# A float32 decoder trunk on one core: the activations of the 256-column matmuls 8 bytes further in SBUF

## The chip, the cores and the metric

The kernel runs on one core of one Trainium2 chip, in one launch. The metric is the device time of an execution in microseconds (us).

## What is computed

Two layers of a decoder trunk work on 256 tokens (S) of width 1,024 (D), in float32. In each layer:

```
h = rmsnorm(x) ;  proj = h @ w_in               (q, k, v of 24 heads of 64, three gates of width 1024)
o_a, o_b, o_c = dilated (12 heads), block (6), stick-breaking (6) attention
merged = g0*(o_a @ w_out_a) + g1*(o_b @ w_out_b) + g2*(o_c @ w_out_c)
x = x + merged @ w_o
x = x + square(relu(rmsnorm(x) @ w_up)) @ w_down      (width 4096)
```

A last RMSNorm follows.

## The kernel before

Every weight matrix is cut on the host into pieces of 128 x 1,024 values (512 KB), 140 for each layer, in the order of their use. SyncE loads them one after the other into four buffers `raw` (line 113). `split_one` (lines 123 to 134) parts each into a high half `wh`, which ScalarE writes (line 132), and a low half `wl`, the rest, which VectorE writes (line 133), six buffers each, three pieces ahead of their use. Activations are parted in the same way into a high and a low half. A product is then three matmuls: low weights by high activations, high by high, and high by low, added up in PSUM in the type float32r.

Three forms of these matmuls stand in the kernel:

- `proj` (lines 208 to 217): the weights are the stationary operand, 128 x 128, and 256 columns of activations (one k-tile of 128 channels, all tokens) stream through. For each of eight k-tiles there are three matmuls, lines 215, 216 and 217. The q, k and gate projections (`qk_pair`, `gate_tile`) read `xh`, the branch projections read `oT`, the projection `w_o` reads `mg`.
- `proj_wide` (lines 219 to 227), in the first half of the MLP: line 223 streams 512 columns (high and low half of `hl` side by side), line 226 streams the 256 of the high half.
- `v_chunk` (line 309) and `down_nat` (lines 668 to 670): the activations are stationary and 512 columns of weights stream.

The activations lie in two slots of 16,384 bytes in each partition, 8 k-tiles x 2 halves x 256 tokens x 4 bytes: a half of a k-tile takes 1,024 bytes. `hilo_slot(i, shift)` (lines 167 to 169) gives a view of slot i that begins `shift` elements behind its start. Slot 0 holds `hl` (shift 0: read by lines 223, 226 and 309) and, between two uses of it, `oT` (shift SHIFT = 16 elements, 64 bytes). Slot 1 holds `xh` and later `mg` (shift 0).

The order in SBUF is fixed by the lines 97 to 102, which allocate the tiles one behind the other: `hl0` (16,448 bytes, with room for the shift), `hl1` (16,384), `skip1` (192, never used), eight `ga` (3,072 each), six `wh` and six `wl` (4,096 each), `V`. The weights therefore begin 33,024 = 129 x 256 bytes behind the start of `hl0` (the `ga` take 96 x 256 more), and every 128 x 128 block of them at a multiple of 256 bytes from it. `hl` lies 0 bytes beyond such a multiple, `oT` 64 bytes, and `xh` and `mg`, at 16,448 = 64 x 256 + 64, also 64.

VectorE and ScalarE write these tiles: `xh` in `normalized` (lines 249 and 250), `oT` in `o_split` (365 and 366), `mg` in lines 599 and 600. Between the projections stand the units of attention; their scores are bursts of small matmuls (line 339), and their products of probabilities and values (line 374 among them) are single ones. The order of the instructions on each engine comes from the order of the program, with priorities for the splits (line 119) and the bursts (line 337).

Of the kernel before, what the change touches and what calls it, by code (L numbers as in the profile page):

```python
# [10 lines left out]
F32 = mybir.dt.float32  # L11
F32R = mybir.dt.float32r
# [3 lines left out]
P = 128  # L16
D = 1024
KT = D // P
S = 256
# [15 lines left out]
RPRI = 1000  # L35
NPRI = 0
NORM_AT = 3
SHIFT = 16
LATE_K = [range(0, 6), range(6, 8)]
BPRI = 400  # L40
QK_BUFS = 6
# [26 lines left out]
def trunk(ctx: ExitStack, tc: tile.TileContext, w, x, norms, gfin, consts, out):  # L68
# [10 lines left out]
    def T(tag, shape, bufs, dt=F32):  # L79
        uid[0] += 1  # L80
        return sp.tile(shape, dt, tag=tag, name=f"{tag}_{uid[0]}", bufs=bufs)
# [5 lines left out]
    def mm_bank():  # L87
        return PS("mm", [P, 512], 2)
# [4 lines left out]
    def t_bank():  # L93
        return PS("t", [P, 512], 2)


    for tag, shape, bufs, dt in (("hl0", [P, KT * 2 * S + SHIFT], 1, F32R),
                                 ("hl1", [P, KT * 2 * S], 1, F32R),
                                 ("skip1", [P, 48], 1, F32),
                                 ("ga", [P, 3, S], KT, F32),  # L100
                                 ("wh", [P, 1024], W_BUFS, F32R), ("wl", [P, 1024], W_BUFS, F32R), ("V", [P, 2, 8, 2, DH], 3, F32R)):
        T(tag, shape, bufs, dt)
# [47 lines left out]
    for o in START:  # L150
        if o[0] == "x":
            d = slice(int(o[1]), int(o[1]) + 2)
# [13 lines left out]

    def hilo_slot(i, shift=0):
        n = KT * 2 * S
        return T("hl%d" % i, [P, n + (SHIFT if i == 0 else 0)], 1, F32R)[:, shift:shift + n].rearrange("p (a b c) -> p a b c", a=KT, b=2)

    def norm_split(hl, nrm, d, on_dve=False):

# [56 lines left out]
    def by_residue(v):  # L229

        return v.rearrange("p (i r) -> p r i", r=DIL)

    hl = hilo_slot(0)
    for d in range(KT):
        norm_split(hl, 0, d, d == 0)

    postponed = []
    for layer in range(DEPTH):
        base = layer * PIECES
        xs = hl  # L240
        xh = hilo_slot(1)

        def normalized():

# [102 lines left out]
        def k_of(f, j, tokens):  # L347
            return QK[f][j * DH:j * DH + DH, 1, tokens]

        oT = hilo_slot(0, SHIFT)  # L350
        last_exp = [None]
        T0, T1, TT = slice(0, P), slice(P, S), slice(0, S)

# [211 lines left out]
        n = base  # L565
# [17 lines left out]
                act.preload_act_table_set("natural_log_exp_and_others")  # L583


        mg = hilo_slot(1)
        for d in range(KT):
            n = base + 60 + d
            st = s_bank()
# [13 lines left out]
        hl = hilo_slot(0)  # L603
        for d in range(KT):
# [6 lines left out]
            p = early[d] if d < 2 else mm_bank() if d % 2 else t_bank()  # L611
# [6 lines left out]
        n = base + 76  # L618
# [101 lines left out]
        hl = hilo_slot(0)  # L720
# [130 lines left out]
```

## Time and profile before

| | us |
|---|---|
| median of 3 runs | 864.6 (862.28 to 864.63) |
| the profiled execution | 864.01 |
| its span, first to last instruction | 862.3 |
| granted clock of TensorE, mean | 0.999 |

A busy share is the part of the span in which an engine works; the chain of work that ended last is followed back from the last instruction, at each step to what released it. For matmuls, which are pipelined, a duration is a latency that overlaps with the next one's; how fast they go one after the other is read from the starts in the timeline. PE is TensorE's matmul row and PEld its weight loads, DVE is VectorE, ACT is ScalarE. L215 is line 215.

### The profile page before, as it was taken

The numbers are of one execution on the slowest core, as the hardware profiler recorded it, in microseconds if no ns is written. First come the engines' busy times: TensorE is split into PE (matmuls) and PEld (weight loads), VectorE is DVE, ScalarE is ACT, GpSimd is POOL, SyncE is SP. The second block draws the span as 40 slices with busy tenths as digits, with TensorE's granted clock in tenths as the row PEclk, the third lists the DMA queues.
The fourth block names the chain that finished last, engine by engine and source line by source line (L and its number), as shares of the span: only waits on it lengthen the run. The fifth ranks groups of instructions, "written<-read, shape, count | busy, mean of one in ns | idle before, by whom it ended". The sixth has DMA issues, their size and how long they took to land.

```text
span 862.3 us, 15138 instructions
## 1 busy us (share of the span) xinstructions
PE 849.8 (99%) x6032; PEld 776.1 (90%) x6032; DVE 628.2 (73%) x958; ACT 468.2 (54%) x681; POOL 21.7 (3%) x36
## 2 busy tenths in 40 slices
PE   8999999999999999999999999999999999999996
PEld 6899999999998888888888999999999988888885
DVE  6977878855887766666578869796567967666664
ACT  6755656658364544444466665666574544444442
POOL 0000100000000000000000101010000000000000
PEclk9999999999999999999999999999999999999999
DMA  8875454554556566566567554445554665566541
GB/s 309 271 222 159 135 164 123 158 172 150 189 195 196 195 188 185 195 190 195 172 175 215 173 157 144 141 132 166 170 172 149 222 215 175 192 193 195 187 133 49
DMA packets 44375, 153.43 MB, mean 178 GB/s; under 512 B 5393, under 2 KB 5777, under 8 KB 44305
## 3 DMA queue, kind: packets, MB, share of 16 engines
q1 hardware_dynamic: 43872, 151.93, 55.9%
q8 instruction: 47, 0.77, 0.4%
q10 hardware_dynamic: 432, 0.54, 0.2%
q14 instruction: 24, 0.19, 0.1%
HBM read 149.31 MB, written 1.05 MB: 174 GB/s over the span
## 4 chain that ended last, share of the span: by engine, by line
PE 93%; DVE 3%; ACT 2%; issue 1%; DMA 1%; SPq 0%; POOLq 0%; DVEq 0%; ACTq 0%
PE mm L223 14%; PE mm L215 11%; PE mm L217 11%; PE mm L216 11%; PE mm L226 7%; PE s L668 7%; PE s L669 7%; PE s L670 7%; PE s L309 5%; PE s L339 2%; PE mm L309 2%; PE s L215 1%; PE s L217 1%; PE s L216 1%; PE t L215 1%
## 5 line engine op out<-in xcount | busy, mean ns | idle before, releaser
L133 DVE TENSOR_TENSOR wl<-raw,wh 128x1024 fp32r<-128x1024 f32 (+1 forms) x281 | 341.6, 1219 | 118.3 <-ACT wh L132 117.5
L132 ACT ACTIVATE wh<-raw 128x1024 fp32r<-128x1024 f32 (+1 forms) x281 | 294.9, 1054 | 238.1 <-PE mm L223 77.3
L215 PE MATMUL mm<-hl,wl 128*128 128x256 f32 x832 | 234.4, 282 | 0.0
L217 PE MATMUL mm<-hl,wh 128*128 128x256 f32 x832 | 233.1, 281 | 0.8 <-DVE hl L250 0.7
L216 PE MATMUL mm<-hl,wh 128*128 128x256 f32 x832 | 233.9, 281 | 0.0
L217 PEld LDWEIGHTS mm<-hl,wh 128*128 128x128 f32 x832 | 156.1, 188 | 1.8 <-DVE hl L250 1.2
L215 PEld LDWEIGHTS mm<-hl,wl 128*128 128x128 f32 x832 | 156.1, 188 | 1.2 <-issue 0.8
L216 PEld LDWEIGHTS mm<-hl,wh 128*128 128x128 f32 x832 | 156.2, 188 | 0.1
L223 PE MATMUL mm<-hl,wh 128*128 128x512 f32 x512 | 129.0, 392 | 0.3 <-DVE wk L640 0.3
L223 PEld LDWEIGHTS mm<-hl,wh 128*128 128x128 f32 x512 | 93.7, 188 | 18.4 <-DVE wk L640 0.5
L668 PE MATMUL s<-wl,ga 128*128 128x512 f32 x256 | 100.4, 392 | 0.0
L669 PE MATMUL s<-wh,ga 128*128 128x512 f32 x256 | 100.0, 391 | 0.0
L670 PE MATMUL s<-wh,ga 128*128 128x512 f32 x256 | 99.0, 389 | 0.0
L226 PEld LDWEIGHTS mm<-hl,wl 128*128 128x128 f32 x512 | 70.4, 190 | 5.3
L640 DVE TENSOR_REDUCE wk<-mm 128x256 f32<-128x512 f32 x64 | 44.0, 691 | 41.7 <-PE mm L226 41.7
L226 PE MATMUL mm<-hl,wl 128*128 128x256 f32 x512 | 72.0, 282 | 0.0
L670 PEld LDWEIGHTS s<-wh,ga 128*128 128x128 f32 x256 | 48.0, 188 | 10.2
L668 PEld LDWEIGHTS s<-wl,ga 128*128 128x128 f32 x256 | 48.2, 188 | 9.8 <-ACT wk L733 0.5
L669 PEld LDWEIGHTS s<-wh,ga 128*128 128x128 f32 x256 | 48.2, 188 | 8.8
L645 ACT ACTIVATE ga<-wk 128x512 fp32r<-128x512 f32 x32 | 20.2, 631 | 66.1 <-DVE wk L642 66.1
L215 PE MATMUL s<-hl,wl 128*128 128x256 f32 x128 | 36.1, 282 | 0.6 <-DVE wk L596 0.6
L216 PE MATMUL s<-hl,wh 128*128 128x256 f32 x128 | 35.7, 279 | 0.0
(153 smaller groups left out, 1001.2 us busy)
## 6 DMA issues: line engine op xcount, KB each, us to landing
raw<-in_w_dram SPq DMA_DIRECT2D x279, 512.0 KB, 3.6
V<-ga SPq DMA_DIRECT2D x32, 64.0 KB, 4.9
xres<-in_x_dram SPq DMA_DIRECT2D x4, 256.0 KB, 5.7
raw<-in_w_dram SPq DMA_DIRECT2D x2, 256.0 KB, 4.0
wk<-in_gfin_dram SPq DMA_DIRECT2D x2, 256.0 KB, 4.0
out_dram<-V SPq DMA_DIRECT2D x2, 256.0 KB, 2.3
out_dram<-V ACTq DMA_DIRECT2D x2, 256.0 KB, 2.1
c_maskA<-in_maskA_dram SPq DMA_DIRECT2D x1, 320.0 KB, 6.8
```

Of the source, the lines that this page charges most:

```text
L132: act.activation(hi[:, c:c + step], r[:, c:c + step], AF.Copy)
L133: dve.tensor_tensor(lo[:, c:c + step], r[:, c:c + step], hi[:, c:c + step].bitcast(F32), op=ALU.subtract)
L215: pe.matmul(dst, lo[:, c:c + P], hl[:, koff + k, 0], start=a, stop=False, skip_group_check=True)
L216: pe.matmul(dst, hi[:, c:c + P], hl[:, koff + k, 0], start=False, stop=False, skip_group_check=True)
L217: pe.matmul(dst, hi[:, c:c + P], hl[:, koff + k, 1], start=False, stop=z, skip_group_check=True)
L223: pe.matmul(bank, hi[:, k * P:k * P + P], hl[:, k].rearrange("p a b -> p (a b)"), start=k == 0, stop=False, skip_group_check=True)
L226: pe.matmul(bank[:, 0:S], lo[:, k * P:k * P + P], hl[:, k, 0], start=False, stop=k == KT - 1, skip_group_check=True)
L309: last_mm = pe.matmul(pv[t], xs[:, k, x_part, t * P:t * P + P], w_part[:, wsl], start=k == 0 and w_part is hi and x_part == 0, stop=k == K ...
L640: dve.tensor_reduce(t[:, a], p[a].rearrange("p (a b) -> p b a", a=2), axis=mybir.AxisListType.X, op=ALU.add)
L668: pe.matmul(dst, uh[:, j % 2, k], lo[:, c], start=j == 0, stop=False)
L669: pe.matmul(dst, uh[:, j % 2, k], hi[:, c], start=False, stop=False)
L670: return pe.matmul(dst, ul[:, j % 2, k], hi[:, c], start=False, stop=j == 2 * npairs - 1)
```

## The change

It gives both slots 128 bytes of room in place of 64 and 0, sets a skip of 128 bytes behind each, and lets `xh`, `oT` and `mg` begin 16 + STEP = 18 elements, 72 bytes, behind the start of their slot. `hl` stays at the start of slot 0. Slot 0 with its skip takes 16,640 = 65 x 256 bytes, slot 1 as much; the weights begin 33,280 = 130 x 256 bytes (and the `ga`) behind the start of `hl0`. So `xh`, `oT` and `mg` lie 72 bytes beyond a multiple of 256 from the weights, and `hl` 0 bytes.

```diff
-SHIFT = 16
+SHIFT = 32
+STEP = 2
...
     for tag, shape, bufs, dt in (("hl0", [P, KT * 2 * S + SHIFT], 1, F32R),
-                                 ("hl1", [P, KT * 2 * S], 1, F32R),
-                                 ("skip1", [P, 48], 1, F32),
+                                 ("skip0", [P, 32], 1, F32),
+                                 ("hl1", [P, KT * 2 * S + SHIFT], 1, F32R),
+                                 ("skip1", [P, 32], 1, F32),
...
     def hilo_slot(i, shift=0):
         n = KT * 2 * S
-        return T("hl%d" % i, [P, n + (SHIFT if i == 0 else 0)], 1, F32R)[:, shift:shift + n].rearrange("p (a b c) -> p a b c", a=KT, b=2)
+        return T("hl%d" % i, [P, n + SHIFT], 1, F32R)[:, shift:shift + n].rearrange("p (a b c) -> p a b c", a=KT, b=2)
...
-        xh = hilo_slot(1)
+        xh = hilo_slot(1, 16 + STEP)
...
-        oT = hilo_slot(0, SHIFT)
+        oT = hilo_slot(0, 16 + STEP)
...
-        mg = hilo_slot(1)
+        mg = hilo_slot(1, 16 + STEP)
```

## Rows read from the trace of the kernel before

**Rows 1.** The page: busy time, granted clock in 40 slices, chain by engine.

```profile
PE 849.8 (99%) x6032; PEld 776.1 (90%) x6032; DVE 628.2 (73%) x958; ACT 468.2 (54%) x681; POOL 21.7 (3%) x36
...
PEclk9999999999999999999999999999999999999999
...
PE 93%; DVE 3%; ACT 2%; issue 1%; DMA 1%; SPq 0%; POOLq 0%; DVEq 0%; ACTq 0%
```

**Rows 2.** Waits of the matmul row: us in total, times, longest.

```profile
PE mm L309 <- ACT wh L132: 2.2, 2, 1.1
...
PE mm L217 <- DVE hl L250: 0.7, 1, 0.7
```

**Rows 3.** Instructions of line 216: duration in ns, least, median and most.

```profile
L216 PEld LDWEIGHTS mm<-hl,wh x832: 187/188/193, 42.2 to 675.6; 128*128 128x128 f32 x167
L216 PE MATMUL mm<-hl,wh x832: 275/279/369, 42.3 to 675.7; 128*128 128x256 f32 x167
...
L216 PE MATMUL s<-hl,wh x128: 278/279/282, 196.4 to 655.7; 128*128 128x256 f32 x128
...
L216 PE MATMUL t<-hl,wh x64: 278/279/280, 219.6 to 672.9; 128*128 128x256 f32 x64
```

**Rows 4.** The page's groups: busy us, mean ns of one.

```profile
L215 PE MATMUL mm<-hl,wl 128*128 128x256 f32 x832 | 234.4, 282 | 0.0
L217 PE MATMUL mm<-hl,wh 128*128 128x256 f32 x832 | 233.1, 281 | 0.8 <-DVE hl L250 0.7
L216 PE MATMUL mm<-hl,wh 128*128 128x256 f32 x832 | 233.9, 281 | 0.0
...
L223 PE MATMUL mm<-hl,wh 128*128 128x512 f32 x512 | 129.0, 392 | 0.3 <-DVE wk L640 0.3
...
L668 PE MATMUL s<-wl,ga 128*128 128x512 f32 x256 | 100.4, 392 | 0.0
```

**Rows 5.** Timeline of the matmul row, 154 to 159: start us, us.

```profile
154.65 0.36 PE L216 MATMUL mm<-hl,wh 128*128 128x256 f32 x1
...
154.97 0.28 PE L215 MATMUL mm<-hl,wl 128*128 128x256 f32 x1
...
158.15 0.28 PE L215 MATMUL mm<-hl,wl 128*128 128x256 f32 x1
158.26 0.28 PE L374 MATMUL t<-ph,V 128*128 128x256 f32 x1
158.38 0.28 PE L216 MATMUL mm<-hl,wh 128*128 128x256 f32 x1
```

**Rows 6.** The same timeline, 115 to 119.

```profile
115.56 0.28 PE L215 MATMUL mm<-hl,wl 128*128 128x256 f32 x1
...
118.28 0.28 PE L215 MATMUL mm<-hl,wl 128*128 128x256 f32 x1
```

**Rows 7.** Groups of the matmul row in the stretch 115.6 to 118.2.

```profile
L215 PE MATMUL mm<-hl,wl 128*128 128x256 f32 x8 | 2.2, 276 | 0.0
L216 PE MATMUL mm<-hl,wh 128*128 128x256 f32 x8 | 2.2, 276 | 0.0
```

**Rows 8.** Timeline of the matmul row, 279 to 283, in the MLP.

```profile
279.29 1.98 PE L223 MATMUL mm<-hl,wh 128*128 128x512 f32 x8
281.10 1.12 PE L226 MATMUL mm<-hl,wl 128*128 128x256 f32 x8
282.05 0.86 PE L223 MATMUL mm<-hl,wh 128*128 128x512 f32 x3
```

**Rows 9.** Instructions of line 226.

```profile
L226 PEld LDWEIGHTS mm<-hl,wl x512: 187/192/192, 252.2 to 844.1; 128*128 128x128 f32 x171
L226 PE MATMUL mm<-hl,wl x512: 274/283/285, 252.4 to 844.2; 128*128 128x256 f32 x171
```

**Rows 10.** Busy us in two stretches: length, PE, PEld, DVE, ACT, POOL, then clock.

```profile
50.00:80.00 30.00, 30.00 (x334) 29.18 (x333) 25.34 (x46) 18.36 (x29) 2.90 (x4) 1.00 0.58 181
140.00:170.00 30.00, 30.00 (x257) 28.99 (x256) 25.73 (x76) 20.43 (x48) 1.22 (x2) 1.00 0.48 158
```

**Rows 11.** Waits of ScalarE.

```profile
ACT wh L132 <- PE mm L217: 50.1, 43, 2.2
```

## The prediction

> **What bounds the kernel now.** I read the page's first, second and fourth parts first. TensorE's matmul row is busy for 99% of the span, the chain of work that ended last lies on it for 93%, and the granted clock is at its full level in every slice, so the clock has nothing to give [rows 1]. The reader should see that the next engine, VectorE, is at 73% and holds 3% of the chain. The waits of TensorE come next: the longest kind sums to 2.2 us [rows 2]. So the time is the number of matmuls times the step from one matmul's start to the next, and only that step can be changed by moving addresses.
>
> The matmuls that the change moves are those of lines 215, 216 and 217: 832 + 128 + 64 on each line by the view of line 216, and as many on the other two lines, 3,072 in all [rows 3, 4]. Each streams 256 columns of activations while the weights of the following matmul are loaded. The recorded duration (about 280 ns) is a pipeline's latency; the step is read from the timeline, and it is there that the argument lies:
>
> - **The ordinary step.** From the start at 154.97 to the one at 158.15 there are 27 steps without a wait: 3.18 us / 27 = 117.8 ns [rows 5].
> - **A shorter step, with the same instructions and the same addresses.** After one matmul of line 374 came between, the same three lines go on from 158.38 [rows 5], and in another such stretch 24 steps take from 115.56 to 118.28: 2.72 / 24 = 113.3 ns [rows 6]. There the matmuls last 276 ns on average [rows 7], against a median of 279 on line 216 as a whole [rows 3].
> - **A longer step where the activations lie at distance 0.** Line 226 multiplies 256 columns too, but reads `hl` of slot 0, which lies a whole multiple of 256 bytes from the weights. Eight steps take from 281.10 to 282.05, 0.95 us. The first can use weights that were loaded under a 512-column matmul; if it takes 113 ns, the other seven take 0.837 / 7 = 119.6 ns [rows 8]. Its median duration is 283 ns, and its weight loads last 192 ns against 188 on line 216 [rows 3, 9].
> - **512 columns.** Eight steps take from 279.29 to 281.10, 226 ns each, twice the 113 ns [rows 8]. So 113 ns is what the stream of 256 columns takes when nothing holds it up, and the ordinary step holds 4.5 ns that are not streaming.
>
> Three steps (113.3, 117.8, 119.6) for one shape at one clock: the load of the next weights and the stream of activations get into each other's way, by an amount that hangs on how the two address sequences meet in time. [...]
>
> **The change part by part.**
>
> *The 8 bytes.* Two of the 256 elements are 2 x 113.3 / 256 = 0.9 ns of the stream. That is how far the stream's place is moved against the weight load. Distances 0 and 64 are the only ones that I find in the trace for these long runs; 72 is not shown, so its step is bounded by the nearest rows: 113.3 ns below, 119.6 ns above. I take the lower end. The reason is rows 5: an interruption by a single matmul moves these lines from 117.8 to 113.3 at unchanged addresses, and they stay there until something interrupts them. The collision is thus one of fine timing, and a shift by a part of a step can end it; a shift that only picks other places in memory while the timing is kept would not show two steps at one distance. That this shift goes the right way I can't read from a row, which is why the other cases keep nearly half the chance.
>
> The sum: 3,072 x (117.8 - 113.3) = 13.8 us if every one changed. Some run at 113.3 already [rows 6], and some stand beside a wait or beside a burst of small matmuls (line 216's mean of 281 against its median of 279 says that there are long ones [rows 3, 4]). I count nine tenths: 12.4 us.
>
> *What is late next.* The weights must be split by ScalarE and VectorE 4% faster. In the stretches with attention VectorE is busy for 25.34 and 25.73 of 30 us [rows 10]; in 4% less time that is 88 to 89%, no bound but little slack. ScalarE's splits on line 132 now wait for line 217 to give back a buffer, 50.1 us in total [rows 11]: the supply runs ahead and this wait shrinks first. I give back 1.5 us of the 12.4 for waits that this cover no longer hides everywhere; the bounds are 0 and 4 us.
>
> *What is written at the new addresses.* ScalarE and VectorE write `xh`, `oT` and `mg` 8 bytes further: 2 x 8 x 3 instructions in each layer, 96 in all. No row shows such a write at this offset. They stand off the chain; the one wait of TensorE on them (line 250) is 0.7 us [rows 2]. Cost 0, bounds half a microsecond either way.
>
> *What is not moved.* `hl` in slot 0 stays at a multiple of 256 from the weights, so lines 223, 226, 309 and 668 to 670 keep their steps. From the start of slot 0 to the weights it is now 33,280 bytes in place of 33,024, another whole multiple of 256; since lines 223 and 668 share a mean of 392 ns although their operands lie in different tiles [rows 4], I count that at 0. The tiles are larger by 256 bytes in a partition in sum, and no instruction touches the two skips. No instruction, transfer or wait is added.
>
> *Sum.* 12.4 - 1.5 = 10.9 us. The profiled execution took 864.0 us (span 862.3 and 1.7 around it), 0.6 below the median of 864.6. 864.0 - 10.9 = 853.1, and against the median 853.7: I say **854 us**.
>
> **The rivals.**
>
> *Nothing changes (0.26).* The step stays at 117.8 ns because the timing settles in the same way after each start, wherever the activations lie. For it: after a matmul that was held up (0.36 us at 154.65) the lines settle at the ordinary step again [rows 5]. Against it: distances 0 and 64 settle at different steps, so the address does enter. The time is 864.6, or a microsecond less or more.
>
> *The two streams meet worse (0.22).* At 72 bytes lines 215 to 217 fall to line 226's step. Place: each of the 3,072; price: nine tenths of them, 2,765 x (119.6 - 117.8) = 5.0 us, so 869.6. It decides as soon as the step passes 118.8, where 2.6 us are lost. For it: the distance 0 shows that an unlucky meeting is stable [rows 8]. Against it: nothing shows a distance that is no multiple of 64. [...]
>
> *The gain is there but halved (within the forecast).* If only every second stretch settles at 113.3, or the step ends near 115.5, the time is 858 to 859; that belongs to the first case's chance.
>
> **How the numbers follow.** A measurement of this kernel can tell 0.3%, 2.6 us, from no change: the line lies at 862.0 and at 867.2. The forecast has 0.52, all of it below 862.0; no change has 0.26, the worse meeting 0.22. The forecast's own range is 851 (all 13.8 us, none given back) to 860. The whole range takes in no change and the worse meeting at its price of 869.6: 851 to 870. What is left out is a step beyond line 226's, and a gain beyond the free stream's.
>
> **What would show it.** Right: long runs of lines 215 to 217 with 113.3 ns between starts, a median duration of 276 ns on line 216, weight loads still at 188; line 226 still at 283 and 512 columns at 389; and the loss of TensorE busy time all in the qk, gate and output projections, none in the MLP. Wrong: a median of 279 (nothing changed), or 282 and more with weight loads of 192 (they meet worse). The forecast also fails if the steps shorten and new waits for lines 132 and 133 before lines 215 to 217 take more than 4 us, or if lines 223 and 226 change their steps, since I hold that only the moved operand matters.

## The result and the profile after

The changed kernel took 873.02 us (median of 5 runs, 872.87 to 873.14) beside 864.6 of before on the same chip: ratio 1.0104, 95% interval 1.009 to 1.0118. It is slower by 1%, where I had forecast 1.2% faster, and it lies above the range of 851 to 870.

The page of the profiled execution (span 871.4 us, 9.1 more than before): busy time, granted clock, and the chain by engine, to be held against [rows 1].

```profile
PE 860.9 (99%) x6032; PEld 787.3 (90%) x6032; DVE 629.2 (72%) x958; ACT 468.1 (54%) x681; POOL 21.3 (2%) x36
...
PEclk9999999999999999999999999999999999999999
...
PE 97%; DVE 1%; DMA 1%; ACT 0%; issue 0%; SPq 0%; POOLq 0%; DVEq 0%; ACTq 0%
```

TensorE is still all there is, at the same clock and with the same number of instructions; it is busy for 11.1 us more, and no other engine for more than 1. The groups say which matmuls (line numbers are two higher now: 217 to 219 were 215 to 217, 225 was 223, 228 was 226, 670 was 668); busy us and mean ns, against [rows 4]:

```profile
L217 PE MATMUL mm<-hl,wl 128*128 128x256 f32 x832 | 238.3, 287 | 0.0
L219 PE MATMUL mm<-hl,wh 128*128 128x256 f32 x832 | 237.7, 287 | 0.7 <-DVE hl L252 0.7
L218 PE MATMUL mm<-hl,wh 128*128 128x256 f32 x832 | 235.3, 283 | 0.0
L225 PE MATMUL mm<-hl,wh 128*128 128x512 f32 x512 | 129.0, 392 | 0.3 <-DVE wk L642 0.3
L670 PE MATMUL s<-wl,ga 128*128 128x512 f32 x256 | 100.4, 392 | 0.0
L228 PE MATMUL mm<-hl,wl 128*128 128x256 f32 x512 | 72.0, 282 | 0.0
```

The three lines whose operand was moved went from 281 or 282 to 283 to 287 ns; the lines that read `hl` or stream weights stand where they stood, to the last digit. The timeline of the matmul row gives the step (start us, us):

```profile
203.09 0.28 PE L217 MATMUL mm<-hl,wl 128*128 128x256 f32 x1
...
205.13 0.28 PE L219 MATMUL mm<-hl,wh 128*128 128x256 f32 x1
```

Seventeen steps in 2.04 us are 120.0 ns, against 117.8 in [rows 5]. Within each three the lines now differ, as the groups of the stretch from 204 to 210 show (mean ns before the second bar):

```profile
L217 PE MATMUL mm<-hl,wl 128*128 128x256 f32 x16 | 4.5, 284 | 0.0
L219 PE MATMUL mm<-hl,wh 128*128 128x256 f32 x16 | 4.5, 284 | 0.0
L218 PE MATMUL mm<-hl,wh 128*128 128x256 f32 x16 | 4.4, 278 | 0.0
```

Over the whole trace I count the steps from the starts of all 3,072 matmuls and set apart those of 128 ns and more, which hold a wait or a change to small matmuls. Before: 2,976 steps of 117.6 ns on average, and 114 of them below 115.5. After: 2,976 steps of 120.8 ns, and one below 115.5. 2,976 x 3.2 ns = 9.5 us; the long steps give back 0.7. All steps of other lines together are 482.8 us before and 483.1 after. So the whole loss lies in the step of the moved matmuls. No wait of the matmul row was added. That of line 309 for ScalarE's split shrank from 2.2 to 1.0 us, and that of line 215 on line 596, 0.6 us before, is gone.

### The profile page after: what moved, and what is told of

Its sections match the earlier page's. It is cut to its first block, busy times and chain, and to the rows that moved or that the text cites. A ratio compares the mean times of both kernels' runs of the same rounds, so it can differ in the third digit from the quotient of the medians.

```text
span 871.4 us, 15138 instructions
## 1 busy us (share of the span) xinstructions
PE 860.9 (99%) x6032; PEld 787.3 (90%) x6032; DVE 629.2 (72%) x958; ACT 468.1 (54%) x681; POOL 21.3 (2%) x36
## 4 chain that ended last, share of the span: by engine, by line
PE 97%; DVE 1%; DMA 1%; ACT 0%; issue 0%; SPq 0%; POOLq 0%; DVEq 0%; ACTq 0%
PE mm L225 13%; PE mm L219 12%; PE mm L217 12%; PE mm L218 11%; PE mm L228 7%; PE s L670 7%; PE s L671 7%; PE s L672 7%; PE s L311 5%; PE s L341 2%; PE s L217 2%; PE mm L311 2%; PE s L219 2%; PE s L218 2%; PE t L217 1%; PE t L219 1%
## 5 line engine op out<-in xcount | busy, mean ns | idle before, releaser
L135 DVE TENSOR_TENSOR wl<-raw,wh 128x1024 fp32r<-128x1024 f32 (+1 forms) x281 | 341.9, 1220 | 123.3 <-ACT wh L134 123.1
L219 PE MATMUL mm<-hl,wh 128*128 128x256 f32 x832 | 237.7, 287 | 0.7 <-DVE hl L252 0.7
L217 PE MATMUL mm<-hl,wl 128*128 128x256 f32 x832 | 238.3, 287 | 0.0
L218 PE MATMUL mm<-hl,wh 128*128 128x256 f32 x832 | 235.3, 283 | 0.0
L218 PEld LDWEIGHTS mm<-hl,wh 128*128 128x128 f32 x832 | 159.4, 192 | 0.1
L219 PEld LDWEIGHTS mm<-hl,wh 128*128 128x128 f32 x832 | 157.4, 189 | 1.7 <-DVE hl L252 1.1
L225 PEld LDWEIGHTS mm<-hl,wh 128*128 128x128 f32 x512 | 93.7, 188 | 18.4 <-DVE wk L642 0.5
L228 PE MATMUL mm<-hl,wl 128*128 128x256 f32 x512 | 72.0, 282 | 0.0
```

The lines of the kernel that those rows point to most:

```text
L135: dve.tensor_tensor(lo[:, c:c + step], r[:, c:c + step], hi[:, c:c + step].bitcast(F32), op=ALU.subtract)
L217: pe.matmul(dst, lo[:, c:c + P], hl[:, koff + k, 0], start=a, stop=False, skip_group_check=True)
L218: pe.matmul(dst, hi[:, c:c + P], hl[:, koff + k, 0], start=False, stop=False, skip_group_check=True)
L219: pe.matmul(dst, hi[:, c:c + P], hl[:, koff + k, 1], start=False, stop=z, skip_group_check=True)
L225: pe.matmul(bank, hi[:, k * P:k * P + P], hl[:, k].rearrange("p a b -> p (a b)"), start=k == 0, stop=False, skip_group_check=True)
L228: pe.matmul(bank[:, 0:S], lo[:, k * P:k * P + P], hl[:, k, 0], start=False, stop=k == KT - 1, skip_group_check=True)
```

## The experiments

The question was what 72 bytes do to the step that 64 don't. Two answers stood against each other at first: that it is the **distance** between activations and weights, by the way in which the two address sequences meet in time (my prediction's reason), or that it is the **place** of the streaming operand alone: the remainder of its start, in bytes, by 16, which is 0 at 64 and 8 at 72. That it should be 16 was a supposition at first; what the step is at each place is shown by the maps alone (means of 118.2, 121.7, 120.3 and 118.1 ns at places 0, 4, 8 and 12, e8_map2). The expectations call the first the meeting or distance theory and the second the place theory. By the line of a place they mean the 16 bytes from one multiple of 16 to the next, a way to name addresses; no run shows a structure of the memory behind it. A third, the layout theory, has it that the new order of the tiles costs the time and the 8 bytes don't. The trunk is the whole kernel. Since the time of the whole kernel mixes many stretches, I also measured the step by itself, in kernels that run only these matmuls.

### A map of the step over the distance

```diff
+WOFFS = [0]
+REPS = 3
...
+    for wo in WOFFS:
+        for o in OFFS:
+            run(p, wo, o)
```

`OFFS` is the list of the distances, 0 to 60 bytes by 4, 64 to 240 by 16 and 248, and back again. `run` issues the three matmuls of lines 215 to 217 for eight k-tiles, REPS times, with the activations `o` and the weights `wo` elements of 4 bytes behind the start of their tiles.

> This kernel leaves out the trunk: it splits one piece of weights and one block of activations, and then runs the three matmuls of lines 215 to 217 for 8 k-tiles, three times over (72 matmuls), at each of 29 distances between activations and weights (0 to 60 bytes in steps of 4, 64 to 240 in steps of 16, 248), up the list and down again; nothing waits. [...] Meeting theory (the step depends on how the two address sequences meet in time): 120 ns at 0, 117.6 at 64, 120.8 at 72 as in the trunk, and other values from 113 to 124 between them that don't go by multiples of 16 alone. If distance did not matter in itself (layout theory), one value of about 117.6 everywhere.

Starts in the timeline of the matmul row, in pairs that are 60 steps apart: at 64 and 112 bytes on the way up, at 8, 4 and 0 on the way down.

```profile
156.64 0.28 PE L102 MATMUL mm<-hl,wl 128*128 128x256 f32 x1
...
163.71 0.28 PE L102 MATMUL mm<-hl,wl 128*128 128x256 f32 x1
...
182.34 0.28 PE L102 MATMUL mm<-hl,wl 128*128 128x256 f32 x1
...
189.14 0.28 PE L102 MATMUL mm<-hl,wl 128*128 128x256 f32 x1
...
489.20 0.28 PE L102 MATMUL mm<-hl,wl 128*128 128x256 f32 x1
...
496.40 0.28 PE L102 MATMUL mm<-hl,wl 128*128 128x256 f32 x1
...
497.87 0.29 PE L102 MATMUL mm<-hl,wl 128*128 128x256 f32 x1
...
505.27 0.29 PE L102 MATMUL mm<-hl,wl 128*128 128x256 f32 x1
...
506.72 0.28 PE L102 MATMUL mm<-hl,wl 128*128 128x256 f32 x1
...
513.92 0.28 PE L102 MATMUL mm<-hl,wl 128*128 128x256 f32 x1
```

7.07 us / 60 = 117.8 ns at 64, 6.80 / 60 = 113.3 at 112, 120.0 at 8, 123.3 at 4 and 120.0 at 0. These are the steps of [rows 5, 6, 8] and one worse. (72 was not in this list; the later maps have it.) The other distances, over the last 59 steps of each stretch: 4, 20, 36 and 52 bytes have 123.4, 122.3, 121.1 and 120.0 ns; 8, 24, 40 and 56 have 120.0, 120.0, 119.9 and 117.8; 12, 28, 44 and 60 all have 117.6 to 117.8. The multiples of 16 scatter from 113.3 to 120.0, and some have two values: 192 was 117.8 on the way up and 113.3 on the way down, with nothing changed but what ran before. Neither answer covers this alone: places 4, 8 and 12 have values of their own, but place 12 costs no more than many at place 0.

### The same map with the weights moved too

```diff
-WOFFS = [0]
+WOFFS = [2]
```

> The same map, but the weights too begin 8 bytes further, so that the distance is 8 less than the offset of the activations. [...] Meeting theory: the same curve against the distance, moved by 8 bytes: 117.6 ns at offset 72 (distance 64), 120 ns at offset 8 (distance 0).

The weights begin two elements, 8 bytes, further. Where the two answers differ, the place wins. Offset 20 (distance 12) has 121.1 ns; the first map had 122.3 at offset 20 and 117.7 at distance 12. Offset 12 (distance 4) has 117.7, against 117.7 at offset 12 and 123.4 at distance 4. The other offsets that are no multiple of 16 come within 1.3 ns of the first map at the same offset, but for 40 and 56, which differ from it by 1.9 and 2.2. At the multiples of 16 the values moved, by up to 7 ns: there the distance matters as well (96 had 120.0 in the first map, here 113.3 on the way up and 120.0 on the way down). Offset 48 (distance 40) had 113.3 on both ways.

### The offset back to 64, and on to 80, in the kernel

```diff
-STEP = 2
+STEP = 0      (e3_step0)
+STEP = 4      (e4_step4)
```

> The changed kernel with the offset set back from 72 to 64 bytes, all else of the new layout kept (room, skips, slot 1 and the weights 192 and 256 bytes further). [...] Layout theory: it stays near 873 us.

863.26 us beside 863.1, ratio 1.000 (0.9991 to 1.001), steps of 117.6. The new layout, with slot 1 and the weights further away, costs nothing; the 8 bytes alone are the change.

> The changed kernel with 80 bytes in place of 72: the next multiple of 16. [...] Meeting theory: not bound to that; the value that the first map gives for 80, between 855 and 875 us.

867.91 us beside 863.1, ratio 1.0053 (1.0036 to 1.007), steps of 119.2 on average. So the place alone does not give the step: 80 and 64 are both at place 0, and 80 is slower. The map had 120.0 there.

### Place 12 and place 4

```diff
-STEP = 2
+STEP = 3      (e7_76: 76 bytes)
+STEP = 1      (e9_68: 68 bytes)
```

> The changed kernel with 76 bytes in place of 72, which too begins inside a 16-byte line. [...] The place within the line decides, as in the first map (12, 28, 44 and 60 bytes all near 117.7 ns, 8, 24 and 40 near 120): about 117.7 ns and 864.5 us within 2.

864.67 us in a single run beside 864.03, steps of 117.7: 76 is no multiple of 16 either, and it loses nothing against 64. So there is no one price for every start off a multiple of 16.

> The changed kernel with 68 bytes in place of 72: the place inside a 16-byte line is 4. Place theory: slower still, since the maps have a mean of 121.8 ns at place 4 (120 to 124): 2,976 steps x (121.8 to 123.4 less 117.6) = 12 to 17 us over before, 876 to 881 us. Distance theory, in which the place in a line means nothing: no such order; a value between 113 and 124 that fits none of 72, 76 and 80 better.

872.89 us in a single run beside 863.77, steps of 121.0. The order (68 and 72 slow, 76 as 64) is that of the place; the size is below the 876 to 881 that I expected, since the trunk's stretches did not settle at the map's worst values.

### The maps again, with interruptions

```diff
+    for again in range(2):
+        for o in range(0, 64, 4):
+            for piece in range(3):
+                for n in range(4):
+                    pe.matmul(p[:, S:S + 64], wh[:, n * P:n * P + P], hl[:, 0:64], start=True, stop=True, skip_group_check=True)
+                run(p, 0, o, 1)
```

This second part runs every multiple of 16 bytes, three times and twice over, each time 24 matmuls behind four small ones of 64 columns.

> The first map for 64 to 128 bytes in steps of 4 and for 192, up and down, and then every multiple of 16 from 0 to 240 twice, each three times for 24 matmuls behind four small ones of 64 columns. Place within the line: about 120 ns at 72, 88, 104 and 120, 117.7 at 76, 92 and 108, over 120 at 68 and 84. In the second part, if the rhythm hangs on how a stretch begins, 24 matmuls at one distance have several values; 112 is of use to the trunk only if it stays near 113 to 115 there.

By a slip the list of distances went to the weights too, so that the first part ran every one of 18 offsets of the activations against every one of 18 of the weights, 1,296 stretches of 72 matmuls. That gives more than was asked. Mean steps in ns by the place of the activations, over all places of the weights (from the 21st matmul of a stretch on; the first three stretches left out):

```
place  stretches  mean   least   most
  0       431     118.2  113.3  123.4
  4       287     121.7  120.0  124.1
  8       287     120.3  117.8  123.3
 12       288     118.1  116.6  122.2
```

The place of the weights makes no such order (for each place of the activations, the means at place 0, 4, 8 and 12 of the weights agree within 0.7 ns). Each place of the activations met all four places of the weights, so the table parts the place from the distance. Only place 0 ever has 113.3, in 24 of 431.

In the second part, with interruptions, the last 20 steps of each stretch give this: 112 bytes had 115.0 to 115.3 ns in six of six, 192 had 113.5, 114.0 and 117.8, 64 had 117.8 in all six, 80 had 118.5 to 120.0, and the other multiples of 16 lay between 116.7 and 120.0. This orders the trunk's results: 64 at 117.6, 80 at 119.2, and the next two.

### 112 and 192 bytes in the kernel

```diff
-STEP = 2
+STEP = 12     (e5_112)
+STEP = 32     (e11_192, with more room and larger skips)
```

> The changed kernel with 112 bytes in place of 72. The first map held 113.3 ns at 112 on both ways through the list. If the map carries over to the trunk: about 2,900 of the 3,072 steps fall from 117.6 to 113.3, 12 us less than before, 851 to 854 us. If the trunk's interruptions throw the matmuls into another rhythm each time (the map had two values at 96 and 192), a mixture: 855 to 866 us.

856.23 us beside 864.03, ratio 0.9919 (0.9902 to 0.9935): the mixture, and not the 851 to 854 of a map carried over whole. 2,282 steps are below 115.5 ns, the mean is 114.6. The groups, and the longest waits of the matmul row:

```profile
L217 PE MATMUL mm<-hl,wl 128*128 128x256 f32 x832 | 232.5, 280 | 0.0
L218 PE MATMUL mm<-hl,wh 128*128 128x256 f32 x832 | 232.2, 279 | 0.0
L219 PE MATMUL mm<-hl,wh 128*128 128x256 f32 x832 | 231.2, 279 | 0.9 <-DVE hl L252 0.8
```

```profile
PE mm L311 <- ACT wh L134: 2.1, 2, 1.2
PE s L217 <- DVE wk L598: 1.2, 4, 0.4
```

Means of 279 and 280 against 281 and 282 in [rows 4]; the wait of line 215 on line 596 (now 217 and 598) is 1.2 us. The steps of 128 ns and more sum to 22.9 us, against 21.3 before: the weights keep up, and 1.5 us come back as waits and changes.

> The changed kernel with 192 bytes in place of 72 (place 0 of a line; room and skips larger). The first map held 117.8 ns on the way up and 113.3 on the way down there. Map carried over: a mixture, 852 to 866 us. Place theory alone bounds it from above only: not slower than before by more than a few us, since place 0 has a mean of 118.2 in the maps.

859.29 us beside 863.77, ratio 0.9947 (0.9932 to 0.9962): 1,493 steps below 115.5 and the rest near 117.6, the mixture that the map had.

### hl moved too

```diff
-    hl = hilo_slot(0)
+    hl = hilo_slot(0, 16 + STEP)      (three places, STEP = 12)
```

> As the run before, and hl too lies 112 bytes beyond a multiple of 256. If the map holds for line 226 (256 columns, 512 of them, at 120 ns), these fall to about 113.5: up to 3 us less than the run before. If what matters on line 226 is something else than the distance, no change against the run before, within 1 us.

857.24 us, 1.0 more than with `hl` at 0, where I had expected up to 3 less or no change. Line 226's step does fall, from 120 to 117.0, which is 1.5 us; but line 223's mean step rises from 229.8 to 231.6 (512 of them, 0.9 us), and line 309, where `hl` is the stationary operand, from 227 to 233 in the greater part. What is gained with one form is lost with two others.

### Weights moved in the kernel

```diff
+        o = 2                                              (e10_72_w8: all pieces, STEP = 2)
+        o = 2 if 12 <= n % PIECES < 76 else 0              (e12_48_w8: projections alone, STEP = -4)
         hi = T("wh", [P, 1088], W_BUFS, F32R)[:, o:o + 1024]
         lo = T("wl", [P, 1088], W_BUFS, F32R)[:, o:o + 1024]
...
```

The lines without a sign stand so in both; the tiles of the weights have room for the shift, and two small buffers are fewer.

> The changed kernel, and every piece of weights too lies 8 bytes further, so that the distance is 64 again while activations (and the weights, where they stream) begin at place 8 of a line. Two small buffers are fewer to make room, so only the steps count. Distance theory: lines of the 256-column matmuls back at 117.6 ns. Place theory: they stay at 120 to 121. [...]

877.47 us in a single run beside 863.77. The distance is 64 again, and the steps stay at 120.1 ns: the distance answer falls. The lines that stream weights at place 8, with 512 columns, are slower too. The groups, mean ns against the 392 of line 668 in [rows 4] and, last, against the 392 of line 223 there:

```profile
L672 PE MATMUL s<-wh,ga 128*128 128x512 f32 x256 | 101.4, 396 | 0.0
L671 PE MATMUL s<-wl,ga 128*128 128x512 f32 x256 | 101.3, 396 | 0.0
L673 PE MATMUL s<-wh,ga 128*128 128x512 f32 x256 | 101.1, 397 | 0.0
L226 PE MATMUL mm<-hl,wh 128*128 128x512 f32 x512 | 130.1, 394 | 0.3 <-DVE wk L643 0.3
```

The mean step of lines 668 to 670 (here 671 to 673) is 233 to 235 ns, against 228 to 230 before, and none is below 228, where before the ordinary one was 226 or 227. So streams of 512 columns lose 3 to 7 ns. That this is the place is not shown: their distance to `ga` moved by the same 8 bytes, and line 223 (here 226), whose stream `hl` stayed at place 0 while its stationary weights moved by 8 bytes, went from 229.8 to 231.9 ns.

> Activations at 48 bytes and, for the pieces of the 256-column projections alone, weights 8 bytes further (two small buffers fewer). The maps held 113.3 ns at this distance of 40 bytes with activations at place 0 in six of six stretches. Map carried over: steps near 113.5, 852 to 856 us. If the trunk's interruptions decide: 117 to 119 ns and 862 to 868 us.

855.44 us beside 863.77, ratio 0.9907 (0.989 to 0.9923), the best kernel of this study: 2,587 steps below 115.5 and a mean of 114.1. The matmul row's busy time fell as the step did:

```profile
PE 840.4 (98%) x6032; PEld 766.3 (90%) x6032; DVE 629.5 (74%) x958; ACT 468.0 (55%) x681; POOL 21.6 (3%) x36
```

### The same streams beside shorter loads

```diff
-                pe.matmul(p[:, 0:S], wl[:, c:c + P], ...
+                pe.matmul(q, wl[:, c:c + wide], ...
```

`wide` is 128, 64 and 32 columns of weights; `q` is as many partitions of `p`.

> This kernel leaves out the trunk, as the first map: the three matmuls over and over, 72 at each of 16 distances from 64 to 124 bytes in steps of 4, up and down, with weights of 128 columns, then of 64, then of 32 (a shorter load beside the same stream of 256 columns; nothing waits). Own cost: a stream that begins at place 4 or 8 of a 16-byte line takes longer by itself, so with 32 columns, where the load ends early, steps at place 4, 8 and 12 stay above those at place 0, by 2 ns or more where 128 columns show 120 to 123. Collision alone: with 64 and 32 columns the steps fall to 113.3 ns at every place, and the differences shrink with the load's length. With 128 columns the means of the maps should come again: about 122 at place 4, 120 at 8, 117.7 at 12.

Starts in pairs that are 60 steps apart: first with loads of 128 columns at 72 bytes, then with 32 columns at 68, 72, 76 and 112.

```profile
36.18 0.28 PE L103 MATMUL mm<-hl,wl 128*128 128x256 f32 x1
...
43.38 0.28 PE L103 MATMUL mm<-hl,wl 128*128 128x256 f32 x1
...
576.57 0.28 PE L103 MATMUL mm<-hl,wl 128*32 128x256 f32 x1
...
583.82 0.28 PE L103 MATMUL mm<-hl,wl 128*32 128x256 f32 x1
...
585.26 0.28 PE L103 MATMUL mm<-hl,wl 128*32 128x256 f32 x1
...
592.34 0.28 PE L103 MATMUL mm<-hl,wl 128*32 128x256 f32 x1
...
593.74 0.28 PE L103 MATMUL mm<-hl,wl 128*32 128x256 f32 x1
...
600.80 0.28 PE L103 MATMUL mm<-hl,wl 128*32 128x256 f32 x1
...
670.68 0.28 PE L103 MATMUL mm<-hl,wl 128*32 128x256 f32 x1
...
677.48 0.28 PE L103 MATMUL mm<-hl,wl 128*32 128x256 f32 x1
```

120.0 ns at 72 with the full load; beside loads of a quarter of the columns 120.8 at 68, 118.0 at 72, 117.7 at 76 and 113.3 at 112. Over all distances with 32 columns: place 4 has 120.3 to 121.8, place 8 117.8 to 120.1, place 12 116.6 to 117.8, place 0 113.3 to 117.6. With a full load the same places have 120.6 to 122.7, 118.8 to 121.4, 117.7 to 120.0 and 113.3 to 120.1; place 12, at a mean of 119.3, is above the 117.7 that I had expected. The means at places 0, 4, 8 and 12 are 116.9, 121.9, 120.2 and 119.3 with 128 columns, 116.5, 120.9, 119.8 and 117.6 with 64, and 115.5, 121.0, 119.1 and 117.4 with 32.

The load of a quarter of the columns lasts more than a quarter of the time (mean ns before the second bar):

```profile
L103 PEld LDWEIGHTS mm<-hl,wl 128*128 128x128 f32 x768 | 146.8, 191 | 15.8 <-ACT hl L95 15.8
L103 PEld LDWEIGHTS mm<-hl,wl 128*32 128x32 f32 x768 | 84.2, 110 | 7.2
```

A price that grew with the load's time would thus fall to about six tenths. Over 113.3 ns, the mean price at place 4 goes from 8.6 to 7.7 ns and at place 8 from 6.9 to 5.8: five sixths and more stay. Measured from the mean of place 0 with the same load, place 4 costs 5.0 ns with the full load and 5.5 with the shortest, and place 8 3.3 and 3.6, so that nothing shrinks. So the price at these places does not go by the length of the load. That the stream is slower by itself is the likeliest reading but not shown, since every matmul here has a load beside it, and a fixed price for each load would look the same.

## Why the prediction was wrong

**The step that failed** is the one that chose the end of the range: "I take the lower end." 113.3 ns was the right lower bound, and the sum behind it was sound, but the reason to take it was not. From one interruption that moved the lines from 117.8 to 113.3 ns I read that any shift by part of a step may end the collision. The runs show two things in its place. At place 0 the steps settle anywhere from 113.3 to 123.4 ns, by the distance and by what ran before. The same addresses can have two rhythms (96 bytes in the second map: 113.3 and 120.0), and that is what [rows 5 and 6] show. A stream that begins at place 4 or 8 never had the rhythm of 113.3, in none of the 574 stretches of the large map; its steps are 120 to 122 ns on average. 72 bytes are at place 8. The interruption told of rhythms at place 0, and nothing in the trace told of place 8; the fact that no row showed one should have weighed more than a pattern in time.

**The rival that came true** is the second, "the two streams meet worse": the sign, and that it falls on each of the moved matmuls, are as it had them. Its reason, the meeting of the two address sequences, is not borne out: at 72 bytes the place decides and not the distance (e8_map2, e10_72_w8). As far as the sign rested on the meeting, it came true by luck. Its price was too small: I took line 226's 119.6 as the end, 1.8 ns on 2,765 steps; measured are 3.2 ns on 2,976. The stretches at 113.3 are lost as well (114 steps before, one after), and 120.8 lies beyond line 226. With that the range's upper end of 870 was too low.

**The first rival's reason**, that the address does not enter, falls with 68, 72, 80, 112 and 192 bytes, which all left 117.6 ns (121.0, 120.8, 119.2 and 114.6 on average, and at 192 a mixture with 1,493 steps below 115.5). With the layout alike, 64 and 72 bytes have 117.6 and 120.8 ns (e3_step0 against the changed kernel). My own reading of the three steps, that the load of the next weights and the stream get into each other's way, is not shown for places 4 and 8: with loads of 110 ns in place of 191 most of the price stays there (e13_load).

**What held.** The neighbours: lines 223, 226, 309 and 668 to 670 kept their steps, the layout cost nothing (e3_step0), the writes at the new addresses cost nothing that shows (the one wait on them is 0.7 us in both). Of the sign for a worse meeting, 282 ns and more on line 216 with weight loads of 192, only the loads came true there; lines 215 and 217 did go from a median of 279 to 284 (217 and 219 now):

```profile
L218 PEld LDWEIGHTS mm<-hl,wh x832: 187/192/193, 42.5 to 684.7; 128*128 128x128 f32 x167
L218 PE MATMUL mm<-hl,wh x832: 278/279/371, 42.6 to 684.8; 128*128 128x256 f32 x167
...
L217 PE MATMUL mm<-hl,wl x832: 278/284/387, 42.5 to 684.7; 128*128 128x256 f32 x167
```

The median of line 216 itself stayed at 279, the very number that I had given for no change: one line of the three is not the group. And what a step of about 113 ns would bring was sized well, at 12.4 us less 1.5 given back, though at other addresses. e12_48_w8 has 114.1 ns and gains 8.3 us (863.77 to 855.44) with 2.6 us more in the long steps (23.9 against 21.3).

**Still open** is why a stream that begins at place 4 or 8 is slower at all, why place 12 costs so little beside places 4 and 8, and what fixes the rhythm at place 0; the runs only list it. No run streams without weight loads. Whether the better rhythm of 112 bytes would last in a kernel with other interruptions was not tried.

## What to carry to other kernels

Where TensorE streams float32 operands back to back and the step between starts is longer than the best step seen for that shape, begin the streaming operand at a multiple of 16 bytes (in the large map the only starts with a step of 113.3 ns; those 4 and 8 bytes behind one had means of 121.7 and 120.3) and sweep its distance to the weights (113.3 to 123.4 ns at such starts). With such starts the distances tried in this kernel were worth from -0.9% (40 bytes, e12_48_w8) to +0.5% (80 bytes), all for 256 columns and loads of 128. Sweep them in a small kernel that interrupts the stream as the real one does, since one set of addresses can have several rhythms (192 bytes in the first map: 113.3 and 117.8 ns): the interrupted map met the trunk's four mean steps (64, 80, 112 and 192 bytes) within 0.6 ns, the clean one missed 192 by up to 2.3. Judge such a change by the step between starts, line by line, and not by the median duration of one line.

## What the runs showed of the hardware that was not expected

- A stream of 256 float32 columns takes a step of 113.3 ns at best, 120.0 to 124.1 if it begins 4 bytes behind a multiple of 16, 117.8 to 123.3 at 8 bytes and 116.6 to 122.2 at 12, as mean steps of 1,293 stretches (e8_map2).
- The place of the stationary operand made no such difference for 256 columns: the means for its four places agree within 0.7 ns (e8_map2).
- 192 bytes had steps of 113.3 and of 117.8 ns in one kernel, with nothing changed but the matmuls that ran before; once settled, each kept on to the end of its stretch (e1_map).
- Streams of 512 columns lost time too when the weights moved by 8 bytes (e10_72_w8): steps of 233 to 235 ns against 228 to 230 where the weights stream (lines 668 to 670), and 231.9 against 229.8 where they are stationary and the stream is at place 0 (line 223). Place and distance are not parted there.
- Loads of 128, 64 and 32 weight columns last 191, 136 and 110 ns; the price of places 4 and 8 over place 0 was 5.0 and 3.3 ns with the longest and 5.5 and 3.6 with the shortest (e13_load).
